# Two-layer decoder trunk: layer 0's last MLP slabs, half-depth tiles and wide quads, and layer 1's memory keys and values moved ahead of k

## The chip, the cores and the metric

The kernel runs on one core of a Trainium2 chip, in one launch. The metric is the device time of that launch in microseconds, the median of three runs. The engines are TensorE (PE in the profile; PEld is its weight load), VectorE (DVE), ScalarE (ACT), GpSimd (POOL) and SyncE (SP, which issues most DMAs).

## The reference, cut to what matters

256 tokens, model width 2048, MLP width 8192, two layers. All values are float32.

```
layer 0:  u = rms_norm(x) @ w_in[0]          # pooling mixer (1536) and memory query (512)
          x = x + concat(pooled, mem_attention) @ w_out[0]
          x = x + squared_relu(rms_norm(x) @ w_ff1[0]) @ w_ff2[0]
shared:   k1, k2, v = rms_norm(x) @ w_kv      # from x after layer 0's MLP
layer 1:  q1, q2, mem_q = rms_norm(x) @ w_in[1]
          differential attention over k1, k2, v; memory attention over
          rms_norm(mem) @ w_mem_kv[1]         # needs mem only, not x
          x = x + concat(both) @ w_out[1]
          x = x + squared_relu(rms_norm(x) @ w_ff1[1]) @ w_ff2[1]
```

Two facts are used below. `w_mem_kv[1]` is applied to the normed memory, so its product does not wait for layer 0. And `z = squared_relu(...)` of width 8192 is the depth of the product with `w_ff2`: 64 blocks of 128 deep, and 16 blocks of 128 columns of output.

## The kernel before, in words

**Numbers.** Each float32 operand is split into a high part in a rounded format and the low rest. A product is three matmuls: high x high, low x high, high x low. Weights come from memory as blocks of 128x128 in the order of use; `Feed` loads them (L141), ScalarE casts the high part into `hi_ring` (L177), and VectorE subtracts to get the low part in `lo_ring` (L180). The rings hold six slots of 512 columns. Preparation runs three entries ahead of use (`AHEAD`), loading three transfers ahead (`LOADS`). Four raw buffers hold plain weights.

**Four ways to spend TensorE on a block.** `a_part` keeps the weight block stationary and streams all 256 tokens, high and low side by side (512 columns), then the low weights with 256 columns. `c_tile` does the same as three matmuls of 256 columns into one half bank. `wide_step` takes a quad of four blocks as the moving operand (512 columns) and the activations as the stationary one, for two halves of the tokens: six matmuls. A **slab job** is part of a fast scheme with seven products where a plain one needs eight: a slab is 2 blocks deep and 1024 output columns wide (half of the model width: g = 0 is the right half, g = 1 the left), works on the two halves of the tokens, and accumulates seven PSUM banks. A slab has four jobs, of 2, 1, 2 and 2 products, three matmuls of 512 columns each. The weight sums that it needs are made by VectorE (L219, L205) and by accumulating DMAs that GpSimd issues (`add_right`, L152). The sums of activations are made in `convert`.

**Layer 0's and layer 1's MLP** (`ffn`). 64 up tiles of 16 blocks make z; z has room for 16 of the 64 blocks at a time. Slab jobs are mixed into the up tiles by a hand-written list of due times in tiles (`early`, `tiles_at`); `due` runs those whose time has come and whose inputs are there. Since the seven banks serve both halves, groups of four slabs of one half alternate with four of the other, and `swap` copies the banks out and in. There are 56 slabs: all 32 of the right half, and 24 of the left. After the left half's last slab `close_left` forms its four quarter results, `scale_rows` scales them, and `turn_left` turns them with transposes into the residual between later up tiles.

After the 64 up tiles twelve jobs are left. `last` then runs eight down tiles of the left half, each over the last 16 blocks of z (128 blocks with `a_part`), with the twelve jobs between their quads for the first six tiles. `finish_banks` closes the right half, and its four `turn`s come in the last two tiles.

**Behind layer 0.** Each finished residual chunk is split into `x_kv` at once (`resid_done`). Then come k (three wide tiles of 16 quads), v (three), layer 1's memory keys and values (`mk1`, `mv1`, two wide tiles), and the queries. The memory is reloaded and split into `mems1`, a tile of its own, during k and v (`mem_again`), in raw buffers shared with the weights.

Emission is by ticks: `at(d, fn)` runs a function d ticks later, and a tick comes after each quad of weights. Each engine takes its instructions in the order in which they stand, so this sets the order on VectorE and ScalarE. PSUM has seven tagged banks for the products ("mm" three, "s" two, "o", "t") and "st" for tiles.

Of the kernel before, what the change touches and what calls it, by code (L numbers as in the profile page):

```python
# [17 lines left out]
P = 128  # L18
# [82 lines left out]
class Feed:  # L101
# [191 lines left out]
def program(ctx, tc, plan, dry, xT, memT, par, lam, cst, wst, yT):  # L293
# [149 lines left out]
    def c_tile(ps, w, l, n, ks, xs):  # L443

        for i, k in enumerate(ks):
            hi, lo = feed.block((w, l, k, n, 1))
# [8 lines left out]
    def wide_step(ps, what, xs, k):  # L455
# [10 lines left out]
        else:  # L466
            for t in range(2):
                nc.tensor.matmul(ps[t], x[t][1], hi, start=k == 0, stop=False)  # L468
                nc.tensor.matmul(ps[t], x[t][0], hi, start=False, stop=False)  # L469
                nc.tensor.matmul(ps[t], x[t][0], lo, start=False, stop=k == NK - 1)  # L470
# [239 lines left out]
    def later_square(n):  # L710

        if n == 0:
# [18 lines left out]
    def ffn(l, xs, tags, done):  # L731
# [22 lines left out]
        z_done, sit_done, summed_up = set(), set(), set()  # L754
        z_free = {j: True for j in range(NK)}
# [182 lines left out]
        left = {}  # L938
        turns = []

        def close_left(j):
# [9 lines left out]
            elif j == 2:  # L951
# [3 lines left out]
                add(left["c12"], left["c12"], banks[4])  # L955
            else:
# [3 lines left out]
                add(u, u, banks[6])  # L960
            for p in of_job[j]:
                restore(p, 0)
            if j == 3:
# [84 lines left out]
        def one_job():  # L1048
# [6 lines left out]
            if end and s + 1 < len(slabs):  # L1055
                if g == 1 and i == 23:
# [8 lines left out]
        def due(tiles, least=0):  # L1065
            n = 0
            while len(jobs) > 12:
                if jobs[0][0] > tiles and (n >= least or not ready(*jobs[0][1:])):
                    break
# [20 lines left out]
        assert len(jobs) == 12 and not turns  # L1090
# [23 lines left out]
        return last  # L1114
# [224 lines left out]
    x_in = []  # L1339
    down = ffn(0, fx, ("S1", "S0"), lambda n: resid_done(n, [(x_in[0], G_KV)], False))  # L1340
# [18 lines left out]
    mems1 = sp.tile([P, NK, 512], F32R, tag="S1", name="mems1")  # L1359

    def mem_again(p):
        t = wp.tile([P, 4, T], F32, tag="raw", bufs=4, name="memraw1")
        nc.sync.dma_start(t, memT[:, 4 * p : 4 * p + 4, :])
        for k in range(4):
            at(
                6 + 2 * k,
                lambda k=k: split_gain(mems1[:, 4 * p + k, :], t[:, k, :], gcol(G_MEM + 16 + 4 * p + k)),
            )

    for p in range(4):  # L1370
        at(46 + 9 * p, lambda p=p: mem_again(p))

# [5 lines left out]
    def pair_of_banks(c, name):  # L1378
        if c % 2:
            return [pp.tile([P, 512], F32, tag="s", bufs=2, name=name) for _ in range(2)]  # L1380
        return [mmt(name) for _ in range(2)]

    c1 = []
    at(12, lambda: c1.extend(columns("x")))
# [22 lines left out]
    ps = pair_of_banks(0, "mk1")  # L1407
    b_tile(ps, "w_mem_kv", 1, 0, mems1)
    mrow1 = key_rows(ps, mem_c, P)
    ps = pair_of_banks(1, "mv1")  # L1410
    b_tile(ps, "w_mem_kv", 1, 1, mems1)
    cat1 = sp.tile([P, NK, 512], F32R, tag="S1", name="cat1")

    mk1_lo = cat1[:, 12:16, 0:T]
    mv1_lo = cat1[:, 12:16, T : 2 * T].rearrange("p h (a d) -> p h a d", a=2)
    mv1 = tp.tile([P, 2, 512], F32R, tag="rows", bufs=3, name="mv1")
    mk1 = tp.tile([P, 4, T], F32R, tag="rows", bufs=3, name="mk1")
    for t in range(2):
        four = "p (h d) -> p h d"
        hi, v4 = mv1[:, t, :].rearrange(four, h=4), ps[t].rearrange(four, h=4)  # L1420
        split_rows(hi, mv1_lo[:, :, t, :], v4, mem_c[0][:, t : t + 1])
    for i in range(2):
        c = slice(2 * i, 2 * i + 2)
        at(
            2,
            lambda i=i, c=c: turn_rows(mrow1, 2 * i, mk1[:, c, :], gcol(G_MK + 1), mk1_lo[:, c, :]),
        )

# [238 lines left out]
```

## Time and profile before

| | |
|---|---|
| median of 3 runs | 1997.1 us (1997.1 to 1997.63) |
| profiled execution, own time | 1997.11 us |
| its span, first to last instruction | 1995.3 us |
| granted TensorE clock | 1.000 |
| TensorE busy | 1990.6 us (100%) |
| VectorE busy | 1716.3 us (86%) |
| ScalarE busy | 1497.9 us (75%) |
| GpSimd busy | 246.7 us (12%) |

The busy times are of one execution. TensorE's matmuls overlap in the trace, since their ends are modelled: the distance from start to start says what one costs. Layer 0's last up tile ends at 862.66 us, k begins at 923.28 us, and the memory keys and values stand from 1057.07 to 1100.59 us.

### The profile page before, as it was taken

How to read it: one execution, taken by the hardware profiler on the slowest of the kernel's cores; microseconds unless marked ns; L12 is line 12 of the kernel's file. 1: busy time of each engine (PE TensorE's matmuls, PEld its weight loads, DVE VectorE, ACT ScalarE, POOL GpSimd, SP SyncE). 2: the span in 40 equal slices, each digit the busy share in tenths (PEclk: the TensorE clock that was granted, in tenths of full speed). 3: DMA queues.
4: the chain of work that ended last, by engine and by line, in shares of the span. 5: the costliest groups of instructions: out<-in, count | busy, mean ns of one | idle time of the engine just before them, and what ended most of it. 6: DMA issues, size and time to landing. Idle time of an engine off the chain costs nothing.

```text
span 1995.3 us, 32048 instructions
## 1 busy us (share of the span) xinstructions
PE 1990.6 (100%) x10534; PEld 1704.2 (85%) x10534; DVE 1716.3 (86%) x3089; ACT 1497.9 (75%) x2792; POOL 246.7 (12%) x291
## 2 busy tenths in 40 slices
PE   9999999999999999999999999999999999999999
PEld 8888888888888888888888889888888888888888
DVE  8888878989989899989765698878889898999987
ACT  7765577787887878778665699567787878878775
POOL 0001311111111111110000000311111111111110
PEclk9999999999999999999999999999999999999999
DMA  9556567888888888765566534657888888888775
GB/s 320 174 191 192 189 199 213 225 229 235 227 232 223 226 236 231 220 188 181 189 232 196 172 127 138 200 190 208 228 219 234 230 227 225 227 234 235 218 216 145
DMA packets 142727, 420.10 MB, mean 211 GB/s; under 512 B 16096, under 2 KB 18784, under 8 KB 142560
## 3 DMA queue, kind: packets, MB, share of 16 engines
q1 hardware_dynamic: 110160, 359.32, 55.6%
q0 software_dynamic: 32256, 58.73, 17.4%
q8 instruction: 82, 1.34, 0.3%
q14 instruction: 85, 0.70, 0.1%
q10 hardware_dynamic: 144, 0.01, 0.0%
HBM read 415.90 MB, written 2.10 MB: 209 GB/s over the span
## 4 chain that ended last, share of the span: by engine, by line
PE 100%; DVE 0%; issue 0%
PE x_bank L434 25%; PE x_bank L436 12%; PE p L867 9%; PE p L869 9%; PE p L870 9%; PE wo L434 6%; PE wo L436 3%; PE u L434 2%; PE ff L434 2%; PE u L436 1%; PE q L468 1%; PE k L468 1%; PE q L470 1%; PE q L469 1%; PE k L469 1%; PE v L468 1%
## 5 line engine op out<-in xcount | busy, mean ns | idle before, releaser
L177 ACT CAST hi_ring<-raw 128x512 fp32r<-128x512 f32 x1001 | 613.4, 620 | 270.8 <-PE x_bank L434 69.9
L180 DVE TENSOR_TENSOR lo_ring<-raw,hi_ring 128x512 fp32r<-128x512 f32 x1001 | 687.1, 695 | 121.8 <-ACT hi_ring L177 105.8
L434 PE MATMUL x_bank<-fx,hi_ring 128*128 128x512 f32 x1952 | 610.1, 394 | 0.0
L436 PEld LDWEIGHTS x_bank<-fx,lo_ring 128*128 128x128 f32 x1952 | 366.6, 188 | 83.6
L436 PE MATMUL x_bank<-fx,lo_ring 128*128 128x256 f32 x1952 | 383.5, 278 | 0.0
L434 PEld LDWEIGHTS x_bank<-fx,hi_ring 128*128 128x128 f32 x1952 | 319.8, 189 | 24.1
L177 ACT CAST hi_ring<-room 128x1024 fp32r<-128x1024 f32 x224 | 235.9, 1053 | 128.2 <-PE p L869 107.4
L180 DVE TENSOR_TENSOR lo_ring<-room,hi_ring 128x1024 fp32r<-128x1024 f32 x224 | 274.0, 1223 | 37.6 <-ACT hi_ring L177 29.1
L180 DVE TENSOR_TENSOR lo_ring<-slab,hi_ring 128x512 fp32r<-128x512 f32 (+1 forms) x224 | 213.9, 955 | 60.4 <-ACT hi_ring L177 59.9
L177 ACT CAST hi_ring<-slab 128x512 fp32r<-128x512 f32 (+1 forms) x224 | 185.8, 830 | 40.3 <-PE p L869 23.9
L867 PE MATMUL p<-hi_ring,sit 128*128 128x512 f32 x448 | 175.5, 392 | 0.0
L869 PE MATMUL p<-hi_ring,sit 128*128 128x512 f32 x448 | 175.1, 391 | 0.0
L870 PE MATMUL p<-lo_ring,sit 128*128 128x512 f32 x448 | 174.3, 389 | 0.0
L152 POOL DMA_DIRECT2D room<-in_w x112 | 96.7, 864 | 556.2 <-DVE lo_ring L180 435.3
L152 POOL DMA_DIRECT2D slab<-in_w x112 | 96.9, 865 | 529.1 <-DVE lo_ring L180 513.0
L434 PE MATMUL wo<-cat,hi_ring 128*128 128x512 f32 x512 | 161.7, 397 | 0.0
L867 PE MATMUL p<-hi_ring,z 128*128 128x512 f32 x336 | 132.1, 393 | 0.0
L869 PE MATMUL p<-hi_ring,z 128*128 128x512 f32 x336 | 131.2, 390 | 0.0
L870 PE MATMUL p<-lo_ring,z 128*128 128x512 f32 x336 | 130.8, 389 | 0.0
L436 PEld LDWEIGHTS wo<-cat,lo_ring 128*128 128x128 f32 x512 | 95.9, 188 | 22.3
L436 PE MATMUL wo<-cat,lo_ring 128*128 128x256 f32 x512 | 101.0, 278 | 0.0
L870 PEld LDWEIGHTS p<-lo_ring,sit 128*128 128x128 f32 x448 | 84.1, 188 | 18.6
(373 smaller groups left out, 3372.5 us busy)
## 6 DMA issues: line engine op xcount, KB each, us to landing
raw<-in_w SPq DMA_DIRECT2D x500, 512.0 KB, 4.4
slab<-in_w SPq DMA_DIRECT2D x112, 512.0 KB, 4.7
room<-in_w SPq DMA_DIRECT2D x112, 256.0 KB, 4.7
slab<-in_w POOLq DMA_DIRECT2D x112, 256.0 KB, 6.6
room<-in_w POOLq DMA_DIRECT2D x112, 256.0 KB, 5.8
memraw<-in_mem SPq DMA_DIRECT2D x5, 512.0 KB, 4.4
resid<-in_x SPq DMA_DIRECT2D x8, 256.0 KB, 5.8
out_y<-resid SPq DMA_DIRECT2D x16, 128.0 KB, 1.9
```

Of the source, the lines that this page charges most:

```text
L152: self.nc.gpsimd.dma_start(t, self.wst[h, :, 0:512], accum_op=ALU.add)
L177: self.last_cast = self.nc.scalar.copy(hi, src)
L180: low = self.nc.vector.tensor_sub(lo, src, hi.bitcast(F32))
L434: nc.tensor.matmul(ps, hi, xs[:, k, :], start=first and c == 0, stop=False)
L436: nc.tensor.matmul(ps[:, T : 2 * T], lo, xs[:, k, 0:T], start=False, stop=last and c == len(ks) - 1,)
L468: nc.tensor.matmul(ps[t], x[t][1], hi, start=k == 0, stop=False)
L469: nc.tensor.matmul(ps[t], x[t][0], hi, start=False, stop=False)
L470: nc.tensor.matmul(ps[t], x[t][0], lo, start=False, stop=k == NK - 1)
L867: nc.tensor.matmul(ps, a[1], hi, start=new, stop=False, **again)
L869: nc.tensor.matmul(ps, a[0], hi, start=False, stop=False, **again)
L870: nc.tensor.matmul(ps, a[0], lo, start=False, stop=end, **again)
```

## The change

Only layer 0's MLP end and the order behind it change; layer 1's MLP keeps the old scheme (`full = l == 0`).

- **Slabs:** 60 in place of 56. The order is now right 24 to 27, left 24 to 27, right 28 to 31. The left half's last 8 blocks of depth stay outside.
- **Due times:** a new early list (`sooner`), 0.8 tiles earlier after that, and 0.95 tiles per slab from slab 50 on, where it was 1.7. A job that is due but has no inputs yet waits.
- **Loads:** a slab's transfer isn't issued while three of its kind are still held.
- **The end** (`last_full`): jobs run up to the last nine; then four half-depth tiles (left columns 4 to 7, `c_tile`, 8 blocks each) and the nine jobs in turns; then eight plain wide quads (left columns 0 to 3).
- **Closing:** the right half is closed job by job with the same function as the left, its last step spread over three ticks; scaling, eight turns of four transposes, and the left half's last additions are each put on a tick of their own, behind the quads and into the memory tiles.
- **Order behind layer 0:** memory keys and values come ahead of k. The memory is reloaded into z itself (`refill`) from the last half-depth tile on. The splits into `x_kv`, the squares and the column sums are put on later ticks.

```diff
@@ Feed.load
+            if r[0] == "S" and sum(x[0] == "S" and x[2] == r[2] for x in self.raw) == 3:
+                return
@@ c_tile: between() ahead of each further quad; wide_step: first and last block given
-    def wide_step(ps, what, xs, k):
+    def wide_step(ps, what, xs, k, ends=(0, NK - 1)):
@@ ffn
-        def close_left(j):
+        def close_left(j, left=left):
...
+            elif left is right:
+                u, v = left["u"], left["v"]
+                add(u, u, banks[5])
+                at(1, lambda: sub(v, v, u))
+                at(2, lambda: add(u, u, banks[6]))
...
-        slabs += [(0, i, False) for i in range(24, 32)]
+        if full:
+            slabs += [(0, i, True) for i in range(24, 28)]
+            slabs += [(1, i, False) for i in range(24, 28)]
+            slabs += [(1, i, True) for i in range(28, 28)]
+            slabs += [(0, i, False) for i in range(28, 32)]
+        else:
+            slabs += [(0, i, False) for i in range(24, 32)]
+        sooner = (4.5, 6, 8, 9.6, 10.6, 11.5, 12.4, 13.4, 14.4, 15.5, 16.5)
...
+            if full:
+                if p < 10:
+                    return sooner[p + 1]
+                return p + 7.6 if p <= 50 else 57.6 + 0.95 * (p - 50)
...
-            if end and s + 1 < len(slabs):
-                if g == 1 and i == 23:
+            if s + 1 == len(slabs):
+                if full:
+                    at(1, lambda: close_left(j, right))
+            elif end:
+                if g == 1 and i == (28 - 1 if full else 23):
                     at(1, lambda: close_left(j))
...
+        def turn_side(side, base, h):
+            t4 = pp.tile([P, 2, T], F32, tag="ot"[h % 2], bufs=1, name="ct")
...   # four transposes
+            c = base + 2 * h
+            nc.vector.tensor_add(resid[:, c : c + 2, :], resid[:, c : c + 2, :], t4)
+
+        def last_full():
+            def some(n):
+                for _ in range(n):
+                    while not ready(*jobs[0][1:]):
+                        tick()
+                    one_job()
+                    tick()
+
+            rest = range(56, 64)
+            some(len(jobs) - 9)
+            for c, t in (("c12", 0), ("v", 1)):
+                scale_rows(left[c], t)
+            for n in range(4, 8):
+                if n == 7:
+                    refill(z)
+                ps = bank()
+                c_tile(ps, "w_ff2", l, n, rest, z, lambda: some(1))
+                def add(n=n, ps=ps):
+                    x = outs[n % 2]
+                    nc.vector.tensor_mul(x[:, 0:T], ps[:, 0:T], r[0])
+                    nc.vector.tensor_add(resid[:, n, :], resid[:, n, :], x[:, 0:T])
+                at(1, add)
+                some(1)
+            some(1)
+            assert not jobs
+            for d, c, t in ((1, "c11", 0), (2, "c12", 0), (4, "v", 1), (5, "u", 1)):
+                at(d, lambda c=c, t=t: scale_rows(right[c], t))
+            for d, side, h in (
+                (6, right, 0), (8, right, 1), (10, right, 2), (11, right, 3),
+                (12, left, 2), (13, left, 3), (14, left, 0), (15, left, 1),
+            ):
+                at(d, lambda side=side, h=h: turn_side(side, 8 if side is right else 0, h))
+            ps = pair_of_banks(0, "ff2")
+            for k in rest:
+                wide_step(ps, ("w_ff2", l, k, 0, 4), z, k % NK, (rest[0] % NK, 63 % NK))
+            def close(t):
+                x = (left["c11"], left["u"])[t]
+                nc.vector.tensor_add(x, x, ps[t])
+                at(1, lambda: scale_rows(x, t))
+            for t in range(2):
+                at(1 + t, lambda t=t: close(t))
@@ behind layer 0
+    def refill(z):
+        mems_in.append(z)
+        def again(p):
+            t = wp.tile([P, 4, T], F32, tag="raw", bufs=RAWS, name="memraw1")
+            nc.sync.dma_start(t, memT[:, 4 * p : 4 * p + 4, :])
...   # four gain splits into z, 7 ticks later for p = 0, else 4
+        again(0)
+        for p, d in ((1, 7), (2, 14), (3, 18)):
+            at(d, lambda p=p: again(p))
...
+    mems1 = mems_in[0]
     for n in range(NK):
-        at(2 + n // 2, lambda n=n: later_square(n))
+        at(20 + n, lambda n=n: split_gain(x_kv[:, n, :], resid[:, n, :], gcol(G_KV + n)))
+        at(9 + n if n < 7 else 24 + n, lambda n=n: later_square(n, n == 0))
+    ps = pair_of_banks(0, "mk1")
+    b_tile(ps, "w_mem_kv", 1, 0, mems1)
+    mrow1 = key_rows(ps, mem_c, P)
+    ps = pair_of_banks(1, "mv1")
+    b_tile(ps, "w_mem_kv", 1, 1, mems1)
...   # splits and turns of memory keys and values, moved with them
-    mems1 = sp.tile([P, NK, 512], F32R, tag="S1", name="mems1")
...
-    at(12, lambda: c1.extend(columns("x")))
+    at(10, lambda: c1.extend(columns("x")))
```

More of the change, by code (lines that the diff above doesn't have):

```diff
@@ L441, in a_part, with c_tile @@
                 tick()
-    def c_tile(ps, w, l, n, ks, xs):
+    def c_tile(ps, w, l, n, ks, xs, between=None):
         for i, k in enumerate(ks):
+            if between and i and feed.pos % 4 == 0:
+                between()
             hi, lo = feed.block((w, l, k, n, 1))
@@ L728, in resid_done, with pair_of_banks, ffn @@
             add_square("x", resid[:, n, :], n == 0)
-    def ffn(l, xs, tags, done):
+    def pair_of_banks(c, name):
+        if c % 2:
+            return [pp.tile([P, 512], F32, tag="s", bufs=2, name=name) for _ in range(2)]
+        return [mmt(name) for _ in range(2)]
+    def ffn(l, xs, tags, done, refill=None):
         z = sp.tile([P, NK, 512], F32R, tag=tags[0], name=f"z{l}")
@@ L960, in close_left @@
                 add(u, u, banks[6])
+            if left is right:
+                return
             for p in of_job[j]:
                 restore(p, 0)
-            if j == 3:
+            if j == 3 and not full:
                 rows = ((left["c11"], 0), (left["c12"], 0), (u, 1), (v, 1))
@@ L1066, in due @@
             n = 0
-            while len(jobs) > 12:
-                if jobs[0][0] > tiles and (n >= least or not ready(*jobs[0][1:])):
+            while len(jobs) > (0 if full else 12):
+                early_one = jobs[0][0] > tiles
+                if early_one and n >= least or (full or early_one) and not ready(*jobs[0][1:]):
                     break
@@ L1089, in ffn @@
         due(64)
-        assert len(jobs) == 12 and not turns
+        assert full or len(jobs) == 12 and not turns
         feed.loads_ahead = LOADS
@@ L1117, in program @@
+        return last_full if full else last
     big = sp.tile([P, 4096], F32, tag="big", name="big0")
@@ L1406, in program @@
     mqg1 = mem_gain(1)
[L1407 to L1427, printed above, removed]
     off = [1024]
```

58 lines of the change are left out of this document (36 added, 22 removed).

## The prediction, made before the change was run

> **What bounds the kernel now.** I read the page first: the busy times and the chain that ended last, then the list of who waited for whom, for TensorE alone.
>
> ```profile
> span 1995.3 us, 32048 instructions
> PE 1990.6 (100%) x10534; PEld 1704.2 (85%) x10534; DVE 1716.3 (86%) x3089; ACT 1497.9 (75%) x2792; POOL 246.7 (12%) x291
> ...
> PE 100%; DVE 0%; issue 0%
> ```
>
> ```profile
> PE warm L375 <- PEq L1640: 0.8, 1, 0.8
> ```
>
> TensorE is the whole chain, and its one wait in the whole trace is 0.8 us before its first matmul. So the time is the number of matmuls times their spacing, and a change pays exactly what it takes off TensorE, less any wait that it brings. The ends of matmuls are modelled, so durations overlap (a 128x512 matmul "lasts" 0.39 us); I price by starts. The timeline of TensorE gives them:
>
> ```profile
> 862.66 0.40 PE L867 MATMUL p<-hi_ring,z 128*128 128x512 f32 x1
> ...
> 864.71 0.62 PE L434 MATMUL x_bank<-z,hi_ring 128*128 128x512 f32 x2
> ...
> 870.28 0.40 PE L867 MATMUL p<-hi_ring,sit 128*128 128x512 f32 x1
> ...
> 873.01 0.62 PE L434 MATMUL x_bank<-z,hi_ring 128*128 128x512 f32 x2
> ...
> 910.38 0.62 PE L434 MATMUL ff<-z,hi_ring 128*128 128x512 f32 x2
> 910.85 0.40 PE L436 MATMUL ff<-z,lo_ring 128*128 128x256 f32 x2
> ...
> 915.96 0.27 PE L1018 MATMUL ct<-const,c_b 128*128 128x128 f32 x1
> ...
> 916.75 0.70 PE L434 MATMUL ff<-z,hi_ring 128*128 128x512 f32 x2
> 917.29 0.40 PE L436 MATMUL ff<-z,lo_ring 128*128 128x256 f32 x2
> ...
> 923.28 0.40 PE L468 MATMUL k<-hi_ring,x_kv 128*128 128x512 f32 x1
> ...
> 999.73 0.39 PE L468 MATMUL v<-hi_ring,x_kv 128*128 128x512 f32 x1
> ...
> 1003.14 1.03 PE L601 MATMUL tr<-const,krow 128*128 128x128 f32 x8
> ...
> 1984.96 0.28 PE L449 MATMUL ff<-z,hi_ring 128*128 128x256 f32 x1
> ...
> 1987.47 0.28 PE L449 MATMUL ff<-z,hi_ring 128*128 128x256 f32 x1
> ```
>
> Five prices follow. **A block of a plain down tile** (`a_part`): 16 blocks from 910.38 to 915.96, 0.349 us each. **A matmul of a slab job**: 12 from 870.28 to 873.01, 0.2275; a slab has 7 products of 3 matmuls, so 4.78 us for the 16 blocks that would cost 5.58 plainly. **A wide quad** (`wide_step`, 6 matmuls): 15 matmuls from 999.73 to 1003.14, 0.2273, so 1.364. **A block of a half-depth tile** (`c_tile`, 3 matmuls of 256 columns): 21 matmuls from 1984.96 to 1987.47, 0.1195, so 0.359. **Eight transposes**: 0.79 from 915.96 to 916.75, and the next pair of matmuls is late by 0.07 (0.54 to 917.29, against 0.47 from 910.38 to 910.85).
>
> A test of the prices: from the last up tile's end (862.66) to the first matmul of k (923.28) are 60.62 us. The parts there, 128 plain blocks (44.6), 12 slab jobs of 63 matmuls (14.3) and 16 transposes (1.7), sum to 60.7. Nothing is lost there.
>
> **The change: what it takes off TensorE.** Before, layer 0 has 56 slabs and 128 plain blocks (8 tiles, 16 deep). After, 60 slabs; of the left half's last 8 k-blocks, tiles 4 to 7 are half-depth tiles (32 blocks) and tiles 0 to 3 are eight wide quads.
>
> - out: 128 x 0.349 = 44.6
> - in: 4 slabs x 4.78 = 19.1; 32 x 0.359 = 11.5; 8 x 1.364 = 10.9; together 41.5
> - transposes: 32 as before, but in eight groups of four, where before there were four of four and two of eight; two more switches at 0.07, so 0.15
>
> The gain is 3.1 - 0.15 = 2.95 us. Bounds: with the half-depth blocks at the plain price and no switch cost it would be 3.4; with 0.07 at each of the sixteen switches between jobs, half-depth tiles and quads (the trace shows none: 9 job matmuls from 862.66 to 864.71, right behind a tile, are 0.228 apart) it would be 1.8. I take 2.95, as its rows are the same shapes in this kernel.
>
> [...]
>
> Memory keys and values of layer 1 (two tiles of 16 quads, 2 x 16 x 1.364 = 43.6 us) only move ahead of k: same matmuls, same 32 weight quads. They cover what stood ahead of k before: the closing of the sums, the turns, and the splits of the shared-key input.
>
> **What could be late instead.** All else must stay behind TensorE. VectorE is the nearest:
>
> ```profile
> core 0: us, PE busy (x) PEld busy (x) DVE busy (x) ACT busy (x) POOL busy (x), PEclk, DMA share, GB/s
> 760.00:800.00 40.00, 40.00 (x210) 34.04 (x209) 38.40 (x63) 32.23 (x54) 6.04 (x7) 1.00 0.84 236
> 862.66:890.00 27.34, 27.34 (x146) 23.44 (x145) 24.64 (x44) 20.48 (x35) 2.59 (x3) 1.00 0.69 178
> 890.00:923.28 33.28, 33.28 (x193) 29.05 (x192) 31.70 (x60) 24.90 (x47) 0.86 (x1) 1.00 0.53 174
> ```
>
> VectorE was 96% busy for 40 us with TensorE full, so such a load alone costs nothing. ScalarE is at 81% there and 75% in the tail, and has room. VectorE's prices, again by starts:
>
> ```profile
> 610.53 0.68 DVE L180 TENSOR_TENSOR lo_ring<-raw,hi_ring 128x512 fp32r<-128x512 f32 x1
> 611.13 0.29 DVE L793 TENSOR_TENSOR room<-stage 128x128 f32<-128x128 f32 x1
> 611.34 0.28 DVE L794 TENSOR_TENSOR room<-stage 128x128 f32<-128x128 f32 x1
> ...
> 611.74 1.22 DVE L180 TENSOR_TENSOR lo_ring<-room,hi_ring 128x1024 fp32r<-128x1024 f32 x1
> 612.88 0.28 DVE L796 TENSOR_TENSOR room<-stage,room 128x128 f32<-128x128 f32 x1
> ...
> 866.91 0.42 DVE L776 TENSOR_TENSOR z<-stage,z 128x256 fp32r<-128x256 f32 x1
> 867.25 0.68 DVE L219 TENSOR_TENSOR room<-room,slab 128x512 f32<-128x512 f32 x1
> ...
> 869.85 0.68 DVE L804 TENSOR_TENSOR sit<-room,sit 128x512 fp32r<-128x512 f32 x1
> ...
> 918.49 1.69 DVE L330 SCALAR_TENSOR_TENSOR x_kv<-resid,param,x_kv 128x256 fp32r<-128x256 f32 x4
> ```
>
> That is 0.60 for 512 columns, 1.14 for 1024, 0.34 for 256 (866.91 to 867.25), 0.21 for 128, 0.40 for a gain split. A slab needs 3 x 1.14 + 3 x 0.60 = 5.2 (three splits of 1024, one of 512, two sums): more than its 4.78 on TensorE. A tile needs four quads, two 256s, and half of a 512 with four 128s: 3.8 against 5.58.
>
> *Up tiles.* The new due times start jobs some 0.8 tile earlier, and from slab 50 on put one slab to 0.95 tile where there were 1.7. Per such pair VectorE has 0.95 x 3.8 + 5.2 = 8.8 for TensorE's 0.95 x 5.58 + 4.78 = 10.1, 87%. No cost.
>
> *Tail, from the last up tile's end to the last plain quad.* By the due times step 56 of the job order ends at 64.01 tiles and step 57 begins at 64.25, so 13 jobs are left when the 64 tiles are through. TensorE: 3.25 slabs 15.5, half-depth 11.5, quads 10.9, two turns 1.0: 38.9 us. VectorE: 13 jobs 16.7, less the three prepared ahead (3.5); 16 quads 9.6; the last up tile's conversion 2.1; left closing's last step 1.8; right closing 4.2; four half-depth tiles' scale and add 2.7; seven splits of the memory 2.8; two turns 1.2: 37.7, or 97%. Just under, with three preparations (some 4 us of TensorE) as cushion. I take 0.2 us, bounds 0 and 4: the 4 is the cushion drained once.
>
> *Readiness.* In the trace the last tile's low part is out at 866.91 + 0.42 and its sums at 869.85 + 0.68, 4.7 and 7.9 us after 862.66. The first job that reads them now comes 9.0 us after (four jobs 4.78, one half-depth tile 2.87, one job 1.37), the first that reads the sums 19.6 after. No cost.
>
> *Gate to the last job.* A slab's third job lets GpSimd add onto the tile that the fourth reads. Before, for the last slab:
>
> ```profile
> 891.52 1.23 DVE L180 TENSOR_TENSOR lo_ring<-room,hi_ring 128x1024 fp32r<-128x1024 f32 x1 [0.46 <-ACT hi_ring L177]
> 893.04 0.86 POOL L152 DMA_DIRECT2D room<-in_w  x1 [8.96 <-DVE lo_ring L180]
> 895.17 0.39 PE L867 MATMUL p<-hi_ring,sit 128*128 128x512 f32 x1
> 899.32 1.05 ACT L177 CAST hi_ring<-room 128x1024 fp32r<-128x1024 f32 x1 [0.41 <-ACT later L717]
> 900.44 1.21 DVE L180 TENSOR_TENSOR lo_ring<-room,hi_ring 128x1024 fp32r<-128x1024 f32 x1
> ```
>
> ```profile
> raw<-in_w SPq DMA_DIRECT2D x18, 512.0 KB, 4.2
> room<-in_w POOLq DMA_DIRECT2D x3, 256.0 KB, 3.9
> ```
>
> ```profile
> room<-in_w POOLq DMA_DIRECT2D x112, 256.0 KB, 5.8
> ```
>
> The first two rows of transfers are the tail's (860 to 925), the last is the page's. Need: 1.52 from split to issue, 3.9 to land, 2.33 for both casts: 7.75 us from the split's start. Given: the split began 3.65 ahead of its job (891.52, 895.17), and to the fourth job there are now 1.37 + half a tile 1.44 + one job 1.37 = 4.17: 7.8. It fits by a hair at the tail's 3.9 and is 1.9 us late at the page's 5.8. The tail's row is the nearest, as loads thin out there too: 0, bounds 0 and 1.9.
>
> *Banks.* The plain quads hold two "mm" banks of three, and memory keys want two: the second is free only when VectorE has added the quads' first bank. TensorE has 6 matmuls (1.37) to go meanwhile, the add takes 0.60; cost 0, up to 1 if VectorE is behind.
>
> *SP.* The four reloads of the memory are issued from the seventh half-depth tile on, each in a raw buffer behind the weights' loads in SP's queue; 18 loads landed in a median of 4.2 us there before, each reload has at least four quads (5.4 us) until its first split, and the quads are prepared three ahead. Cost 0.
>
> Sum: 1995.3 - 2.95 + 0.2 = 1992.55 of span. The profiled execution took 1997.11, 1.8 more than its span and 0.01 above the median of 1997.1, so 1994.4. That is 0.14% off; 0.2% (4.0 us) is about what a measurement of this kernel can tell from no change, so the forecast itself lies within it.
>
> **Rivals.**
>
> 1. *A short new wait in the tail.* The third-to-fourth-job gate at 5.8 us (1.9), the cushion emptied (up to 4), or both banks late (1). For it: 97% and a margin of 0.05 us; against it: 96% passed without a wait. 1995.5 to 1999.3, the middle 1996.5.
> 2. *Slower: the turns queue on VectorE.* Eight turns now come nearly one to a quad, over two banks; each needs the add of the turn two before, which stands in VectorE's order behind splits, closings and memory splits. If VectorE enters them more than 3 us late (two quads with their turns are 3.8, less the add), TensorE waits at each turn, a quad's splitting and the add together, some 1 us, 8 times; the gates ahead of it must have cost the cushion of 4 already. 1994.2 + 8 = 2002.2, and up. Against it: after the quads VectorE has 11.6 for 14.1 of TensorE, so a lag shrinks.
> 3. *No gain, as jobs aren't ready.* If the last jobs are held back, they run without cover: TensorE waits the 7.9 us of the chain above less what jobs stand between; at 9.0 and 19.6 this needs a chain twice as long. At twice the chain (16 us against 9.0) it is some 6 us: 2000.
> 4. *Faster by over 0.2%*, under 1993.1: the bound above gives 3.4, and there is no wait in the trace to remove. Only if shapes in turns pack closer than either alone.
>
> **Chances.** Forecast, within 1993.6 to 1995.5: 0.52. Rival 1: 0.24. Rival 3: 0.04. Rival 2: 0.16. Rival 4: 0.04. Faster 0.04; same 0.52 + 0.24 + 0.04 = 0.80; slower 0.16. The range leaves out rivals 2 and 3 and nearly all of rival 4, and reaches past both bounds of the forecast and of rival 1: 1993.4 to 1999.5, about 0.77.
>
> **What would show it.** Right: 60 slabs' worth of job matmuls (1260 in layer 0), 48 of the wide and 96 of the 256-column shape under the down weights, no TensorE wait over 0.3 us between the last up tile and k, and k's first matmul about 2.95 earlier once the 43.6 us of memory tiles are taken off. Wrong: TensorE idle before L867 of the last fourth job (the gate), before the first wide quads (VectorE's cushion), or before transposes into the "o" and "t" banks (rival 2); or VectorE under 90% there with a wait all the same, which would point to a transfer or a bank.

## The result, and the profile after

| | before | after |
|---|---|---|
| median | 1997.2 us (1997.04 to 1997.72, 22 runs) | 2000.91 us (1999.36 to 2003.04, 22 runs) |
| profiled execution, own time | 1997.11 us | 2003.04 us |
| its span | 1995.3 us | 2001.2 us |

The ratio is 1.0019, with a 95% interval of 1.0012 to 1.0025: slower by 0.19%, which is small but clear of noise, and 1.4 us above the predicted range. The forecast, 1994.4, is 6.5 us under the median. The profiled execution of the changed kernel is the slowest of its 22; nine of them, from 2001.62 us up, had a mean granted clock of 0.999, and the other 13, up to 2001.19, had 1.000.

The page after, in the lines that answer to those of before:

```profile
span 2001.2 us, 31948 instructions
PE 1992.0 (100%) x10506; PEld 1701.5 (85%) x10506; DVE 1715.1 (86%) x3083; ACT 1502.4 (75%) x2808; POOL 253.4 (13%) x299
...
PE 97%; DMA 1%; DVE 1%; ACT 1%; issue 0%; SPq 0%; ACTq 0%; DVEq 0%
```

The chain is no longer all TensorE. TensorE's waits, one group to a line (total, times, longest):

```profile
PE mk L472 <- DVE room L1200: 2.3, 1, 2.3
PE x_bank L454 <- DVE lo_ring L182: 0.9, 1, 0.9
PE tr L605 <- DVE krow L540: 0.8, 1, 0.8
PE warm L377 <- PEq L1732: 0.8, 1, 0.8
PE p L877 <- ACT hi_ring L179: 0.5, 1, 0.5
```

The third stands at 62.79 us, at the start of layer 0 and ahead of everything the change touches; of the executions profiled here, this one alone has it. So I count from the first up-tile matmul of layer 0 to that of layer 1: 1068.0 us before, 1072.5 after, 4.5 more. The other three waits lie in these 4.5. TensorE's timeline has all of them, and a fourth, shorter one:

```profile
885.70 0.40 PE L879 MATMUL p<-hi_ring,sit 128*128 128x512 f32 x1
886.95 0.39 PE L454 MATMUL x_bank<-z,lo_ring 128*128 128x256 f32 x1 [0.86 <-DVE lo_ring L182]
...
892.57 0.51 PE L880 MATMUL p<-lo_ring,sit 128*128 128x512 f32 x1
893.60 0.50 PE L877 MATMUL p<-hi_ring,sit 128*128 128x512 f32 x1 [0.52 <-ACT hi_ring L179]
...
924.05 0.48 PE L472 MATMUL mk<-hi_ring,z 128*128 128x512 f32 x1
924.36 0.40 PE L473 MATMUL mk<-hi_ring,z 128*128 128x512 f32 x1
924.60 0.39 PE L474 MATMUL mk<-lo_ring,z 128*128 128x512 f32 x1
924.83 0.49 PE L1153 MATMUL ct<-const,room 128*128 128x128 f32 x3
927.65 0.79 PE L472 MATMUL mk<-hi_ring,z 128*128 128x512 f32 x1 [2.33 <-DVE room L1200]
928.25 0.63 PE L473 MATMUL mk<-hi_ring,z 128*128 128x512 f32 x1
928.67 0.63 PE L474 MATMUL mk<-lo_ring,z 128*128 128x512 f32 x1
...
930.38 0.58 PE L472 MATMUL mk<-hi_ring,z 128*128 128x512 f32 x1
930.80 0.39 PE L473 MATMUL mk<-hi_ring,z 128*128 128x512 f32 x1
```

Start to start and beyond the shapes' spacing, TensorE loses 1.02 us at 886, 0.80 at 893, 0.20 at the last slab's fourth job (908.5), and 2.49 ahead of 927.65, in the first tile of layer 1's memory keys. Behind that last wait the next seven matmuls start some 0.43 us apart instead of 0.2275 (0.60 for the first), another 1.54 us. The windows (length; PE, PEld, DVE, ACT, POOL busy; then the granted clock, the DMA share and GB/s) show why:

```profile
920.00:924.80 4.80, 4.80 (x26) 3.94 (x26) 4.42 (x9) 3.00 (x7) 0.00 (x0) 1.00 0.92 294
924.80:927.60 2.80, 0.52 (x4) 0.25 (x2) 1.69 (x4) 2.34 (x5) 0.00 (x0) 0.96 0.54 218
927.60:928.60 1.00, 0.95 (x2) 0.83 (x3) 1.00 (x2) 0.76 (x2) 0.00 (x0) 0.50 0.51 82
```

The granted clock fell to 0.50. Together 6.05 us were lost, and the stretch is 4.5 longer: without these losses it would be 1.55 shorter, where 2.95 was forecast. The half clock's 1.5 us belong to this execution and not to the median one, whose mean clock of 1.000, by its rounding, leaves room for an estimated 1 us of such a loss at most.

**The first wait (886).** VectorE's timeline; the row that TensorE waits for is the split at 886.22:

```profile
882.68 0.68 DVE L973 TENSOR_TENSOR room<-room,p 128x512 f32<-128x512 f32 x1
...
884.42 0.68 DVE L974 TENSOR_TENSOR stage<-stage,room 128x512 f32<-128x512 f32 x1
885.02 0.68 DVE L221 TENSOR_TENSOR room<-room,slab 128x512 f32<-128x512 f32 x1
885.62 0.68 DVE L975 TENSOR_TENSOR room<-room,p 128x512 f32<-128x512 f32 x1
886.22 0.68 DVE L182 TENSOR_TENSOR lo_ring<-raw,hi_ring 128x512 fp32r<-128x512 f32 x1
```

VectorE has no gap there. The left half's closing (L973 to L975, three times 0.6) and a slab sum stand ahead of the split.

**The second (893).** ScalarE's timeline:

```profile
891.50 0.59 ACT L956 COPY keep<-p 128x512 f32<-128x512 f32 x1 [1.72 <-PE p L880]
891.98 0.63 ACT L811 CAST sit<-room 128x512 fp32r<-128x512 f32 x1
892.50 1.05 ACT L179 CAST hi_ring<-room 128x1024 fp32r<-128x1024 f32 x1
```

The first copy of the right half's closing (L956) waits 1.72 us for TensorE to finish its bank, and the cast that TensorE needs next stands behind it. That the copy is the cause is a reading of this trace; e7_nodma, below, speaks against it.

**The third (927.65).** SyncE, ScalarE and VectorE in order of time:

```profile
891.14 10.96 SPq L143 DMA_DIRECT2D raw<-in_w  x3
910.77 0.33 SPq L1439 DMA_DIRECT2D memraw<-in_mem  x1
915.72 1.31 ACT L414 ACTIVATE z<-memraw,param 128x256 fp32r<-128x256 f32 x3 [1.15 <-DMA memraw<-in_mem]
918.41 0.33 SPq L1439 DMA_DIRECT2D memraw<-in_mem  x1
919.77 7.94 SPq L143 DMA_DIRECT2D raw<-in_w  x4
925.26 1.14 ACT L179 CAST hi_ring<-raw 128x512 fp32r<-128x512 f32 x2 [1.44 <-DMA raw<-in_w]
925.91 0.69 DVE L182 TENSOR_TENSOR lo_ring<-raw,hi_ring 128x512 fp32r<-128x512 f32 x1 [1.37 <-ACT hi_ring L179]
926.92 0.68 DVE L1200 TENSOR_TENSOR room<-room,ff 128x512 f32<-128x512 f32 x1
```

From 902.1 to 910.77 SyncE issued nothing: the memory's reload stands in its order and waits for a raw buffer, and the weights stand behind it (e1_rows, where the reloads take other buffers, issues one at 896.44 and one at 903.45). The weights' load issued at 919.77 lands after 5.4 us and is cast into the ring from 925.26 on, and ScalarE and VectorE both stood still for it. The closing of the quads' first token half (L1200) stands behind that split on VectorE, and it frees the second bank that the memory keys need. TensorE had by then run the first token half of three quads of the keys, and the three second halves follow from 927.65 on.

### The profile page after: what moved, and what is told of

The parts are those of the page before. It is cut to its first block, busy times and chain, and to the rows that moved or that the text cites. A ratio compares the mean times of both kernels' runs of the same rounds, so it can differ in the third digit from the quotient of the medians.

```text
span 2001.2 us, 31948 instructions
## 1 busy us (share of the span) xinstructions
PE 1992.0 (100%) x10506; PEld 1701.5 (85%) x10506; DVE 1715.1 (86%) x3083; ACT 1502.4 (75%) x2808; POOL 253.4 (13%) x299
## 4 chain that ended last, share of the span: by engine, by line
PE 97%; DMA 1%; DVE 1%; ACT 1%; issue 0%; SPq 0%; ACTq 0%; DVEq 0%
PE x_bank L436 24%; PE x_bank L438 12%; PE p L877 9%; PE p L879 9%; PE p L880 9%; PE wo L436 6%; PE wo L438 3%; PE u L436 2%; PE ff L436 1%; PE u L438 1%; PE q L472 1%; PE k L472 1%; PE q L474 1%; PE q L473 1%; PE k L474 1%; PE v L472 1%
## 5 line engine op out<-in xcount | busy, mean ns | idle before, releaser
L179 ACT CAST hi_ring<-raw 128x512 fp32r<-128x512 f32 x985 | 600.3, 620 | 249.6 <-PE wo L436 57.3
L182 DVE TENSOR_TENSOR lo_ring<-raw,hi_ring 128x512 fp32r<-128x512 f32 x985 | 675.0, 693 | 113.0 <-ACT hi_ring L179 98.5
L179 ACT CAST hi_ring<-room 128x1024 fp32r<-128x1024 f32 x232 | 244.4, 1054 | 154.9 <-PE p L879 97.0
L182 DVE TENSOR_TENSOR lo_ring<-room,hi_ring 128x1024 fp32r<-128x1024 f32 x232 | 283.5, 1222 | 61.9 <-ACT hi_ring L179 61.5
L182 DVE TENSOR_TENSOR lo_ring<-slab,hi_ring 128x512 fp32r<-128x512 f32 (+1 forms) x232 | 221.2, 953 | 42.6 <-ACT hi_ring L179 38.2
L877 PE MATMUL p<-hi_ring,sit 128*128 128x512 f32 x464 | 181.8, 392 | 0.5 <-ACT hi_ring L179 0.5
L879 PE MATMUL p<-hi_ring,sit 128*128 128x512 f32 x464 | 181.2, 391 | 0.0
L880 PE MATMUL p<-lo_ring,sit 128*128 128x512 f32 x464 | 179.6, 390 | 0.0
L877 PE MATMUL p<-hi_ring,z 128*128 128x512 f32 x348 | 136.8, 393 | 0.0
L879 PE MATMUL p<-hi_ring,z 128*128 128x512 f32 x348 | 136.1, 391 | 0.0
L880 PE MATMUL p<-lo_ring,z 128*128 128x512 f32 x348 | 135.0, 390 | 0.0
```

Of the source, the lines that this page charges most:

```text
L179: self.last_cast = self.nc.scalar.copy(hi, src)
L182: low = self.nc.vector.tensor_sub(lo, src, hi.bitcast(F32))
L877: nc.tensor.matmul(ps, a[1], hi, start=new, stop=False, **again)
L879: nc.tensor.matmul(ps, a[0], hi, start=False, stop=False, **again)
L880: nc.tensor.matmul(ps, a[0], lo, start=False, stop=end, **again)
```

## Experiments

Five explanations were tried; the letters are those of the expectations. **A:** the reload competes for the weights' raw buffers. **B:** the plain quads hold a bank that the memory keys want. **E:** at the end VectorE and ScalarE have no room, because too many slab jobs stand bare, without a tile between; the order of the closing alone does not matter. **F** (formed after the first runs): a reload issued beside an accumulating transfer slows that transfer, and the last slab's fourth job waits for it. The expectations also weigh C (the two earlier waits alone make up the loss) and D (the order of the closings makes them, the opposite of E). Against all: the TensorE count itself is wrong.

Every median is set beside the kernel before on the same chip (1997.22, 1997.17 or 1997.14).

### The reload in other buffers, and the quads in other banks

`e1_rows` takes the reload out of the weights' raw buffers, `e2_banks` moves the quads from two "mm" banks to the two "s" banks, `e3_both` does both, `e4_early` also starts the reload two half-depth tiles sooner.

```diff
-            t = wp.tile([P, 4, T], F32, tag="raw", bufs=RAWS, name="memraw1")
+            t = tp.tile([P, 4, T], F32, tag="rows", bufs=3, name="memraw1")    # e1, e3, e4
-            ps = pair_of_banks(0, "ff2")
+            ps = pair_of_banks(1, "ff2")                                       # e2, e3, e4
-                if n == 7:
+                if n == 5:                                                     # e4
                     refill(z)
```

> Edit: the four reloads of the memory go into the 'rows' buffers (the slabs' own, free by then) in place of the raw buffers that the weights use; nothing else. Theory A (raw buffers): the reloads take raw buffers, the next weights' transfers are issued late, ScalarE waits for them, and VectorE's closing of the quads' bank stands behind that: the 2.3 us wait ahead of the memory keys and the slow matmuls after it (some 1.4 us) go, and the time falls by 3 to 4.5 to about 1997 (1996.3 to 1998). Theory B (VectorE late in giving the bank free, whatever the transfers): the wait stays within 0.5 us and the time stays at 2000 to 2001.5. Theory C (it is the two waits among the last jobs that cost): time stays within 1 us of 2000.9.

> Edit: the eight plain quads use the two 's' banks in place of two of the three 'mm' banks, so the memory keys need no bank that is still to be closed. Theory A: the weights of the third quad of the keys are late all the same (their cast began 0.35 us after TensorE had run dry); a wait of 1 to 1.7 us stays, perhaps short enough that the matmuls behind it are not slowed: 1998.5 to 2000. Theory B: the wait is gone, 1996.5 to 1997.5. Theory C: 2000 to 2001.5.

> Both edits: reloads in 'rows', quads in the 's' banks. Theory A: as with the reloads' edit alone, within 0.5 us (1996 to 1997.5), as the bank was late only through the transfers. Theory B: as with the banks' edit alone. What stays above 1994.2 is then the waits among the last jobs, some 2 us (theory C's share).

> Both edits, and the reloads begin two half-depth tiles earlier (ahead of the sixth in place of the eighth). Theory A: the reload is no longer in the way, so 0 to 0.5 us off the version with both edits; the earlier splits (four of 0.40 us on VectorE) fall among the last jobs, and if VectorE is what makes TensorE wait there (theory C by VectorE), it is 0.5 to 1.5 us slower than the version with both edits.

| | median us | ratio to before, 95% |
|---|---|---|
| after | 2000.91 | 1.0019 [1.0012, 1.0025] |
| e1_rows | 2002.87 (2002.63 to 2004.36) | 1.0029 [1.0018, 1.0040] |
| e2_banks | 1998.58 (1997.81 to 2000.22) | 1.0008 [0.9999, 1.0017] |
| e3_both | 2002.60 (2001.99 to 2003.90) | 1.0028 [1.0017, 1.0038] |
| e4_early | 2002.85 (2001.44 to 2003.28) | 1.0026 [1.0016, 1.0036] |

B stands as a remedy: with the other banks the wait at 927.65 is gone, and with it the half clock. The median, 1998.58, lies in the interval given for A, but the wait that A would have left is not there. A falls as a remedy. In e1_rows the wait of the memory keys is gone too, but a larger one ends at 911.07, with half clock from about 912.1 to 915.5 behind it (eight matmuls). Its rows, from the waits and the timelines of GpSimd, SyncE and ScalarE in e1_rows:

```profile
PE p L877 <- ACT hi_ring L179: 3.8, 2, 3.0
...
902.78 0.86 POOL L154 DMA_DIRECT2D room<-in_w  x1 [6.42 <-DVE lo_ring L182]
903.45 0.33 SPq L1439 DMA_DIRECT2D memraw<-in_mem  x1
909.98 1.04 ACT L179 CAST hi_ring<-room 128x1024 fp32r<-128x1024 f32 x1 [3.92 <-DMA room<-in_w]
```

With buffers free, SyncE issues a reload 0.67 us after the accumulating transfer, which then lands after 7.1 us instead of 3.8. This is the gate to the last job, priced in the prediction at 3.9 and at most 5.8. In the changed kernel the want of buffers had held the reload back to 910.77, and so kept the gate open. e1_rows, e3_both and e4_early all missed what was expected of them. e3_both loses what e1_rows loses (3.1 us at the gate); with the earlier reload of e4_early the gate costs 1.6, but 1.45, 0.77 and 0.57 are lost in three other places.

### Without the reload, and with it later

`e7_nodma` prices the reload as a whole: it leaves the four transfers out and splits another tile in their place, so layer 1's memory keys and values are of other data. `e8_late` (e3_both as its base) puts the reload behind the last job in the program, with fewer ticks between the reloads and to the first split.

```diff
-            nc.sync.dma_start(t, memT[:, 4 * p : 4 * p + 4, :])
+            t = fx[:, 4 * p : 4 * p + 4, 0:T].bitcast(F32)                     # e7
...
             some(1)
             assert not jobs
+            refill(z)                                                          # e8, in place of n == 7
```

> The changed kernel, its four reloads of the memory left out: the 16 splits into z read another tile that lies there, so VectorE and ScalarE do the same work and only the transfers and their raw buffers are gone (layer 1's memory keys and values are thus of other data). Theory A+B (the reloads delay the weights, the weights delay VectorE, and so the bank): the wait of 2.3 us ahead of the keys and the slow matmuls go, 1996.5 to 1998.5. If the bank's hand-over alone is the cause: 2000 to 2001.5 as before.

> Against the version with both edits (2002.6, TensorE waiting 3.0 us for the last job's weights while an accumulating transfer ran beside a reload): quads in the 's' banks, reloads in the 'rows' buffers, but the first reload is issued only behind the last slab job, so no reload runs beside the accumulating transfer. Theory F (the reload slows the accumulating transfer that gates the last job): the 3.0 us and the slow matmuls behind go, 1997.5 to 1998.8. If the 'rows' buffers themselves are at fault (the reload waiting for a slab's buffer in SP's queue): 2001 or more. If the reloads now come too late for their splits: a new wait among the memory keys, 1999 to 2002.

e7_nodma: 1998.09 (1997.93 to 1998.70), 1.0005 [0.9996, 1.0014]. Without the transfers the wait at 927.65 and the half clock are gone, while 1.02 and 0.93 at 886 and 892 stay. So the reload, as the changed kernel places it, cost 2.8 us of the median, and the two earlier waits have another cause. The second of them, from e7_nodma's ScalarE and TensorE timelines:

```profile
890.08 0.59 ACT L956 COPY keep<-p 128x512 f32<-128x512 f32 x1
...
891.96 0.50 PE L880 MATMUL p<-lo_ring,sit 128*128 128x512 f32 x1 [0.77 <-DVE lo_ring L182]
```

Here the copy waits for nothing, TensorE waits for a split of VectorE, and as much is lost. So the waiting copy of the changed kernel can't be the whole cause.

e8_late missed: 2003.27 (2001.66 to 2004.82), 1.0031 [1.0019, 1.0042]. The order of the program did not bind the issue: the first splits of a reload stand at 889.56, ahead of the last jobs, and a later reload left at 904.22, 0.67 us after the transfer of 903.55, which took 6.9 us. The wait stayed, 2.95.

### The reload behind the transfer, in GpSimd's queue

`e10_pool` issues e8_late's reloads from GpSimd's queue; `e11_behind` also orders them behind the last accumulating transfer there; `e12_behind_pace` adds e6_pace's due times (below).

```diff
-            nc.sync.dma_start(t, memT[:, 4 * p : 4 * p + 4, :])
+            d = nc.gpsimd.dma_start(t, memT[:, 4 * p : 4 * p + 4, :])          # e10, e11, e12
+            feed.order(d, feed.last_add.ins.name)                              # e11, e12
```

> The kernel of e8_late (reloads in the other buffers, quads' bank moved, 2003.27) with the four reloads issued from GpSimd's queue instead of SyncE's, so that they stand behind the last accumulating transfer. In e1_rows, e3_both and e8_late SyncE issued the second reload at 903.45 to 904.22, beside the transfer issued at 902.8 to 903.55, and that landed after 6.9 to 7.1 us instead of 3.8 to 3.9; the wait of 2.95 to 3.1 us followed. If the reload beside the transfer is what makes it slow, the transfer lands after 3.8 to 4.2 us, the wait at the last job is 0.3 to 0.8 us, no matmul behind it runs at half clock, and the median is 1998.0 to 1998.8. If it is the buffers themselves (the other tag's order of use) or the two transfers slowing each other in whatever queue they stand, the transfer takes 6 us or more again and the median stays at 2001.5 to 2003.3.

> The kernel of e10_pool, with the reloads now ordered on GpSimd's queue behind the last accumulating transfer (in e10_pool the first was issued at 885.12 and the second at 899.11, ahead of the slabs' own transfers, so it did not ask its question). If the reload beside the accumulating transfer is what made the last job wait in e1_rows, e3_both and e8_late, the transfer lands in 3.8 to 4.2 us, the wait at that job is at most 0.8 us, no stretch at half clock follows, and the median is 1998.0 to 1998.8 (e2_banks 1998.58). If the buffers' own order is the cause, the wait is 2.7 us or more and the median 2001.5 to 2003.5.

> The kernel of e11_behind with the last tiles paced as in e6_pace. If the two corrections are independent, the waits left are those of e6_pace (0.30 to 0.64 each) or fewer and the median is 1997.0 to 1997.8, no slower than the kernel before (1997.14). If VectorE's and ScalarE's work at the end has no room, a wait comes back at another place, as in e5_spread and e9_later, and the median is 1998.5 to 1999.5.

e10_pool: 2003.76 (2003.06 to 2004.45), 1.0032 [1.0020, 1.0045], and it did not ask its question. Without the order the reloads went ahead of the slab's transfers; GpSimd's and ScalarE's timelines:

```profile
885.12 0.55 POOL L1438 DMA_DIRECT2D memraw<-in_mem  x1 [0.34 <-DVE room L221]
889.73 0.86 POOL L154 DMA_DIRECT2D slab<-in_w  x1 [4.05 <-DVE room L805]
...
891.19 1.71 ACT L414 ACTIVATE z<-memraw,param 128x256 fp32r<-128x256 f32 x4 [2.29 <-DMA memraw<-in_mem]
```

The memory's splits then stood on ScalarE waiting for their data, with the casts behind them: 2.96 us lost on TensorE at 894.88, and half clock from about 894 to 901.

e11_behind: 1998.06 (1997.71 to 1998.49), 1.0005 [0.9996, 1.0014]. It differs from e10_pool by the order alone:

```profile
902.58 0.87 POOL L154 DMA_DIRECT2D room<-in_w  x1 [6.42 <-DVE lo_ring L182]
903.12 1.96 POOL L1438 DMA_DIRECT2D memraw<-in_mem  x3
...
906.68 1.05 ACT L179 CAST hi_ring<-room 128x1024 fp32r<-128x1024 f32 x1 [1.15 <-DMA room<-in_w]
```

Three reloads follow the transfer at once, and it lands after 4.0 us. One reload in SyncE's queue had made it 7.1. F holds here: a reload slowed the transfer from another queue (7.1 us), and three did not from behind it in its own (4.0). The wait at the gate is 0.37, nothing runs at half clock, and the time equals e7_nodma's, which has no reload at all: so placed, the reload costs nothing that can be seen. (The last transfer's name, `feed.last_add`, is kept by `add_right`.)

### The waits at 886 and 893

`e5_spread` and `e6_pace` have e2_banks as their base. e5_spread leaves the work and spreads the closings over more ticks; e6_pace starts the last slabs sooner, so that fewer jobs are left bare behind the last tile. `e9_later` is e6_pace with two of the eight plain quads ahead of the last fourth job.

```diff
-                    at(1, lambda: close_left(j, right))
+                    at(1 if j == 3 else 3, lambda: close_left(j, right))       # e5; the left half's last step spread too
-                return p + 7.6 if p <= 50 else 57.6 + 0.95 * (p - 50)
+                return p + 7.6 if p <= 50 else 57.6 + 0.86 * (p - 50)          # e6, e9, e12
+            quads(rest[:2])                                                    # e9
             some(1)
             assert not jobs
...
+            quads(rest[2:])
```

> Against the version with the quads in the 's' banks (1998.6): the left half's last closing step is spread over three ticks as the right half's is, and the right half's first closing steps stand two ticks later, behind the next casts. Theory D (order on the two splitting engines: a closing step ahead of a split makes TensorE wait, 1.0 us on VectorE and 0.8 us on ScalarE in the trace): both waits go and the time falls by 1 to 2 us, to 1996.6 to 1997.6. Theory E (the four jobs in a row behind the last up tile ask more of VectorE, 5.2 us for 4.8, than it can give, whatever the order): the waits move but their sum stays within 0.5 us, 1998 to 1999.

> Against the version with the quads in the 's' banks (1998.6): from slab 50 on one slab to 0.86 up tiles in place of 0.95, so ten jobs in place of thirteen are left behind the last up tile and no row of four jobs without a tile between. Theory E: the wait of 1.0 us right behind the last up tile goes, unless as much comes back among the up tiles; 1997.3 to 1998.3. Theory D: the left closing moves into the up tiles where there is cover, 1.0 us less; the one on ScalarE (0.8) stays: 1997.3 to 1998. If the up tiles cannot carry the pace (VectorE 88% there), new waits ahead of the last up tile: 1998.5 or more.

> The kernel of e6_pace (quads' bank moved, last tiles paced closer) with two of the eight plain quads moved ahead of the last slab's fourth job, so that its accumulating transfer has two quads' time, 2 x 1.37 = 2.7 us, more. If the last wait left at the gate (0.64 us in e6_pace, 906.61 to 907.48) is the transfer's 3.9 us alone, it is gone: median about 1996.9 against e6_pace's 1997.58, and the reload of the memory, issued at 907.4 there, is not held by it. If the wait is only moved (ScalarE's casts in their row, or VectorE's closing steps now later than the quads), the time stays at 1997.4 to 1998.0. If the later last job makes the closing and the turns late, a wait of 1 us or more shows at the first matmuls of layer 1's keys and the time is 1998.5 or above.

e5_spread: 1999.01 (1998.67 to 2000.12), 1.0009 [1.0000, 1.0018]. The waits change place and sum to as much: 0.49, 0.31, 1.39, 0.33 and 0.23, where e2_banks has 1.03, 0.80, 0.43 and 0.24.

e6_pace: 1997.58 (1997.19 to 1998.17), 1.0001 [0.9993, 1.0010]. The wait of 1.03 is gone; 0.40, 0.30, 0.34 and 0.64 are left. The same work in another mixture of jobs and tiles passes, in the one other order tried (e5_spread) it does not: E holds for the first wait. For the second the cause stays open.

e9_later: 1999.27 (1998.11 to 2000.53), 1.0010 [1.0001, 1.0019], slower than e6_pace, as the worst of its three expected outcomes had it. The wait at the gate is gone, and two others stand in its place:

```profile
PE ct L1153 <- DVE resid L1157: 1.0, 1, 1.0
PE x_bank L452 <- DVE room L1180: 0.8, 1, 0.8
```

e12_behind_pace: 1997.74 (1997.37 to 1998.92), 1.0004 [0.9996, 1.0013], in the interval that independence allowed. Its waits are those of e6_pace (0.40, 0.30, 0.26, 0.67). No version beat the kernel before; e6_pace and e12_behind_pace come nearest, and their intervals hold the ratio 1, as do those of e2_banks, e7_nodma and e11_behind.

## Why the prediction was wrong, point by point

- **What bounds the kernel:** right. TensorE's time is the count times the spacing, and what the result has above that is a wait, a slow clock, or one of the small steps told next.
- **The gain, 2.95 (1.8 to 3.4): the prices held, but not all of it was left.** In the same stretch, taking off the losses named above, the saving is 1072.5 - 6.05 = 1066.45 against 1068.0, so 1.55; in e6_pace it is 1068.05 - 1.68, so 1.63, in e11_behind 1068.64 - 2.18, so 1.54. Set each step from one matmul's start to the next beside the median step of its tile and shape: 111 steps before are longer by 0.03 to 0.15 us, 8.69 us in all, and 128 after, 10.05 us. That is 1.36 more, and 1.55 + 1.36 = 2.91 is the gain that counts and spacings give. The term of 0.15 for switches is not what failed. Behind each group of transposes the first step is long by 0.08 to 0.09, such as 924.05 to 924.36 above, but the step ahead of it is short by as much (0.028 for 0.109), before and after the change. What is new stands elsewhere: eight long steps (0.79) among the last jobs, from 884.88 to 909.27, next to the waits (one of 0.11 behind each, such as 893.60 to 893.94), and five (0.30) in the up tiles. So more than half of the missing 1.4 stands beside the waits. This is a count over traces, not an experiment.
- **Up tiles, no cost:** nearly right. No wait stands ahead of 884.8 in layer 0's MLP, only the five steps of 0.05 to 0.10 just named.
- **Tail on VectorE, 97%, 0.2 us:** the place was right, the size was not. The kernel has 25 products (of 7 to a slab) behind the last up tile, in 14 jobs where the prediction has 13: 3.6 slabs and not 3.25. The first five jobs, nine products in 6.2 us from 878.95 on, run with no tile between, where a slab asks 5.2 us of VectorE for 4.78 of TensorE, and the closing fell among them. VectorE was busy 10.99 of the 11.05 us to 890. An average over the whole tail hid its first quarter. Cost 1.0, within the bounds 0 and 4.
- **ScalarE "has room": not shown to be right.** The second wait cost 0.8, for which no term stood, and in the changed kernel it ended with a cast that stands behind a copy waiting for a bank. But in e7_nodma the copy does not wait and 0.93 is lost at the same place, so the cause of this wait stays open. In e6_pace 0.3 is lost near there (895.38). That a waiting instruction on ScalarE holds up TensorE is clearer in e10_pool: the splits wait 2.29 us for their data, and TensorE loses 2.96.
- **Readiness:** right; no wait on z or its sums in the changed kernel.
- **The gate, 0 (0 to 1.9): right in the changed kernel**, 3.8 us to land and 0.2 lost. But this was luck: SyncE issued nothing beside the transfer, since it waited for a buffer. The 3.9 is the median of three; the very transfer that the prediction shows, issued at 893.04 in the trace before, landed at 898.45, after 5.4 us, with 512 KB of weights issued 0.33 us behind it in SyncE's queue. And the 7.1 us of e1_rows is beyond the range's 5.8, which came from the page's median over all such transfers.
- **Banks (0 to 1) and SP (0): the steps that decided it.** Both looked at their own resource. The median load of 4.2 us was a little short (4.8 in the changed tail, 5.4 for the load of 919.77); what I left out is that a reload waits for a free raw buffer in SyncE's queue and that the weights behind it wait too, and that a late weight holds, in VectorE's order, the addition that frees the bank. Each is needed: other banks alone (e2_banks), or no reload (e7_nodma), and the wait is gone. In the profiled execution it cost 2.5, over the bound of 1, and the half clock behind it 1.5 more, which no term held; in medians the reload cost 2.8 (e7_nodma).
- **Rivals.** Rival 1 was the kind of what happened, a short wait, at 1995.5 to 1999.3; the gate that led its list gave 0.2, the late bank that ended it (1) gave the most, and several waits together passed its upper end. Rival 2 did not come: no turn waited for a bank in the changed kernel (one of 1.1 us did in e9_later). Nor did rival 3.

In medians: 3.7 us slower, of which the reload is 2.8 (e7_nodma). The 0.9 that remain are about the waits left in e7_nodma's profile, 2.2 us, less the 1.55 that is left of the gain.

## What to carry to other kernels

When a queue's transfers need buffers, price a moved transfer by when its buffer is free and by what stands behind it in that queue; then follow each engine's order from the late tile to the bank or buffer that someone else wants, since two costs of zero can make one wait. A share of busy time over a whole stage says little about its first ten microseconds, and on an engine with time to spare one instruction that waits for its data can make TensorE wait (in e10_pool a split on ScalarE waited 2.29 us, with TensorE's casts behind it, and TensorE lost 2.96). Put a price on the pause itself too: a stop of TensorE of 2.33 to 2.96 us brought a granted clock of 0.50 with it in the profiles of the changed kernel, e1_rows and e10_pool, and one of 2.78 in that of e8_late did not.

## What the runs showed of the hardware

**The clock after a short pause.** With TensorE idle for 2.33 us in the changed kernel, 2.96 in e1_rows and 2.68 in e10_pool came a stretch at a granted clock of 0.50, of about 3.4 us in the first two and 6.8 in the third. It did not begin with the first matmul behind the pause: in e1_rows the clock was 1.00 from 911 to 912, though matmuls ran again from 911.07 on, and 0.51 on average from 912 to 915.5. A pause of 2.78 in e8_late's profile had none behind it:

```profile
907.00:911.00 4.00, 1.83 (x6) 0.88 (x6) 1.71 (x2) 0.42 (x1) 0.00 (x0) 1.00 0.50 147
911.00:914.00 3.00, 2.32 (x10) 1.94 (x11) 2.34 (x4) 3.00 (x6) 0.00 (x0) 1.00 0.00 0
```

So the length of the pause alone does not decide, and one kernel has both: of 22 executions of the changed kernel nine had a mean clock of 0.999 and 13 had 1.000; of e8_late's six, five were at 0.998 or 0.999. What else decides, no run here shows.

**One queue against another.** An accumulating transfer of 256 KB landed in 3.8 to 4.0 us with nothing issued in SyncE's queue from 2.1 us ahead of it until it landed (the last one in the changed kernel and in e2_banks), and in 4.0 with 1.5 MB behind it in its own queue (e11_behind). It took 5.3 to 5.4 with 0.5 MB of weights issued some 0.3 us later in SyncE's queue (at 893.04 in the kernel before, at 896.62 in the changed one), and 6.0 to 7.1 with a reload of 0.5 MB issued there some 0.7 us later (e4_early, with a second reload behind it, 6.0, e8_late 6.9, e3_both 7.0, e1_rows 7.1). So it need not be a reload. What stood behind it in its own queue did not slow it measurably: 4.0 us in e11_behind and 3.9 in e12_behind_pace, against 4.0 in e2_banks with nothing behind it.
